# A depthwise convolution whose shared tap sum moves from VectorE to ScalarE and GpSimd

## The chip, the core and the metric

One core of one Trainium2 chip runs the whole model in one launch. The metric is the device time of that launch in microseconds (us). The engines are named as the profile names them: PE (TensorE matmul), PEld (its weight load), DVE (VectorE), ACT (ScalarE), POOL (GpSimd) and SP (which issues the DMAs). Each works through a list of its own in a fixed order and waits where an operand or a buffer is not ready.

## What is computed

A decoder of two layers over 1024 positions of 1024 features. The change lies in the first layer's convolution block. The reference, cut to it:

```
def conformer_conv(h, w_pw1, b_pw1, w_dw, b_dw, ln_g, ln_b, w_pw2, b_pw2):
    u = h @ w_pw1 + b_pw1
    a, gate = jnp.split(u, 2, axis=-1)
    u = a * jax.nn.sigmoid(gate)
    u = depthwise causal convolution of u over time, 31 taps per feature, + b_dw
    u = jax.nn.silu(layernorm(u, ln_g, ln_b))
    return u @ w_pw2 + b_pw2
```

The rest of the model (cross-attention into 256 memory tokens, two MLPs, one attention layer) follows it and is not touched. Some of the cross-attention's preparation depends on weights and memory tokens alone: for each of 2 layers and 4 heads, two products of weight matrices (the code calls the whole `memory_matrices`, this text "prep").

## The kernel before

Features lie on the 128 partitions, positions along the free axis, so the 1024 features make 8 chunks (`m`, `NCH`) and the positions two halves of 512 (`HALVES`).

For each chunk `gated_unit` computes the gate: per half two products of 24 matmuls (the gate's, then the linear part's; f32 numbers are split into a high and a low part, hence three passes over 8 blocks), each into one of the two banks of `pm`. ACT takes the sigmoid of the first (`sg`, L368) and DVE combines it with the second into `u` (L370). A chunk of `u` is stored as even and odd positions (`u[:, 0]`, `u[:, 1]`), with 15 zero columns in front.

`convolve` makes the 31 taps with 512-column instructions, in the form that saves multiplications: with differences `d0`, `d1` of even and odd positions (L393, L394), and one sum that both outputs share,

- `both` = bias + the 16 pair sums of taps times the odd positions: one TENSOR_SCALAR (L396) and 15 SCALAR_TENSOR_TENSORs on DVE (L400), each adding to the one before;
- output half `s=0` (even outputs): `both` + 16 taps over `d0`; `s=1`: `both` + 15 taps over `d1`, all on DVE (L408), accumulated in place in `X[:, m, HALVES[s]]` in SBUF.

The two outputs are added into `acc[0]`, `acc[1]` (L354), whose partition means start the layer norm after the last chunk: `token_mean` and `spread` are small PE products (L158, L167), with DVE, ACT and POOL steps between. Then `linear` multiplies by `pw2` (384 matmuls of 512 columns), and `add_x` (L324) leaves the new residual.

Prep is a generator: `conv_layer` calls it for 4 pieces of work before and 2 more in each chunk. For one head it makes 32 products `mem,praw` (64 matmul records: an f32 product runs as two), 16 `kt,praw` and 8 `praw,vt`, in PSUM banks of its own (`pps`, 4 banks), which ACT empties into `o` tiles (L483, L501; two buffers each) that SP stores to DRAM.

No order is written out by hand in this stage. A scheduler goes through the program in the order in which the code traced it, keeps its own estimate of when operands are ready, and gives each engine the ready instruction that was traced first. The result is a fixed list for each engine.

Of the kernel before, what the change touches and what calls it, by code (L numbers as in the profile page):

```python
# [12 lines left out]
F32 = mybir.dt.float32  # L13
F32R = mybir.dt.float32r
AF = mybir.ActivationFunctionType
ALU = mybir.AluOpType
# [3 lines left out]
P = 128  # L20
D = 1024
S = 1024
NCH = D // P
HALF = 512
# [6 lines left out]
TAPS = 31  # L31
PAD = TAPS - 1
# [4 lines left out]
HALVES = (slice(0, HALF), slice(HALF, S))  # L37
# [49 lines left out]
def trunk(ctx, tc, a, out):  # L87
    nc = tc.nc
    act, dve, pool, pe = nc.scalar, nc.vector, nc.gpsimd, nc.tensor
# [14 lines left out]
    def col(name, i):  # L104
        return par[:, COLS[name] + i : COLS[name] + i + 1]
# [30 lines left out]
    X = open_x()  # L136
    nrm = ctx.enter_context(tc.tile_pool(name="nrm", bufs=2))
# [3 lines left out]
    def bank(p):  # L141
        return p.tile([P, HALF], F32, name="mm", tag="mm")

    def banks(n):
        return tc.tile_pool(name="pm", bufs=n, space=PSUM, reuse_waits="tile")
# [144 lines left out]
        dve.tensor_tensor(X[:, m, sl], t, X[:, m, sl], op=ALU.add)  # L290


    def conv_layer(pm, prep):
        with tc.tile_pool(name="conv", bufs=2) as cp:
            for sl in HALVES:
                next(prep)
# [34 lines left out]
            hs = operands()  # L331
            ahead = gate_weights(0)
            u = padded()
            for sl in HALVES:
                normalize(hs, "mix0", sl)
                next(prep)
                gated_unit(pm, cp, 0, ahead, hs, u[:, :, PAD // 2 :], sl)
            acc = [cp.tile([P, HALF], F32, name=f"acc{s}", bufs=1) for s in range(2)]
            for m in range(NCH):
                if m:  # L340
                    u = padded()
                    for sl in HALVES:
                        gated_unit(pm, cp, m, ahead, hs, u[:, :, PAD // 2 :], sl)
                if m + 1 < NCH:
                    ahead = gate_weights(m + 1)
                for _ in range(2):
                    next(prep, None)

                convolve(cp, m, u, pairs[:, m])
                for s, sl in enumerate(HALVES):  # L350
                    if m == 0:
                        act.copy(acc[s], X[:, m, sl])
                    else:
                        dve.tensor_tensor(acc[s], acc[s], X[:, m, sl], op=ALU.add)  # L354
# [7 lines left out]
    def gated_unit(pm, cp, m, ws, hs, u, sl):  # L362
        sg = cp.tile([P, HALF], F32, name="sg")
        for j, w in zip((1, 0), ws):
            t = bank(pm)
            product(t, by_weights(w, hs, sl))
            if j:
                act.activation(sg, t, AF.Sigmoid, bias=col("pw1_b", NCH + m))  # L368
            else:
                dve.scalar_tensor_tensor(  # L370
                    u[:, :, sl.start // 2 : sl.stop // 2],
                    t.rearrange("p (n s) -> p s n", s=2), col("pw1_b", m),
                    sg.rearrange("p (n s) -> p s n", s=2), op0=ALU.add, op1=ALU.mult,
                )
# [8 lines left out]
        dve.tensor_tensor(sums[:, :, :n], two[:, :, :, 0], two[:, :, :, 1], op=ALU.add)  # L383
        return sums

    def convolve(cp, m, u, sums):


        n, k = S // 2, TAPS // 2
        even, odd = u[:, 0, :], u[:, 1, :]  # L390
        d0 = cp.tile([P, n + k], F32, name="d0")
        d1 = cp.tile([P, n + k - 1], F32, name="d1")
        dve.tensor_tensor(d0, even[:, : n + k], odd[:, : n + k], op=ALU.subtract)  # L393
        dve.tensor_tensor(d1, even[:, 1 : n + k], odd[:, : n + k - 1], op=ALU.subtract)  # L394
        both = cp.tile([P, n], F32, name="both")
        dve.tensor_scalar(  # L396
            both, odd[:, :n], sums[:, 0:1], col("dw_b", m), op0=ALU.mult, op1=ALU.add
        )
        for j in range(1, k + 1):
            dve.scalar_tensor_tensor(  # L400
                both, odd[:, j : j + n], sums[:, j : j + 1], both, op0=ALU.mult, op1=ALU.add
            )
        out = [X[:, m, sl] for sl in HALVES]
        for s, d, taps in ((0, d0, k + 1), (1, d1, k)):
            y = both
            for j in range(taps):
                w = col("dw_w", m * TAPS + 2 * j + s)
                dve.scalar_tensor_tensor(  # L408
                    out[s], d[:, j : j + n], w, y, op0=ALU.mult, op1=ALU.add
                )  # L410
                y = out[s]

# [15 lines left out]
    @contextmanager  # L428
    def prep_pools(n):
        with tc.tile_pool(name="prep", bufs=2) as pp, tc.tile_pool(name="pps", bufs=n, space=PSUM) as pq:  # L430
            yield pp, pq
# [1014 lines left out]
```

## Time and profile before

| | us |
|---|---|
| median of 3 runs (2818.59 to 2823.66) | 2822.05 |
| the profiled execution | 2825.31 |
| its span on the engines | 2823.3 |
| PE busy | 2740.8 (97%) |
| DVE busy | 2030.9 (72%) |
| ACT busy | 1278.3 (45%) |
| POOL busy | 703.1 (25%) |

Times in the trace count from the start of the span. The convolution block takes the stretch from 0 to about 526 us: the last `add_x` starts at 525.5. A busy share is an average over stages with different limits, so the prediction looks at this stretch alone. Of a row that groups instructions, the numbers behind the bar are busy time (us), mean duration (ns), and, behind a second bar, the engine's idle time before them with what ended it. Instructions of one engine can overlap at their ends: busy time divided by count is then below the mean duration.

### The profile page before, as it was taken

What the parts mean: (1) busy time and instruction counts of PE and PEld (TensorE: products, weight loads), DVE (VectorE), ACT (ScalarE), POOL (GpSimd) and SP (SyncE); (2) the same over time, 40 slices, a digit from 0 to 9 for tenths busy, and PEclk for the clock granted to TensorE, in tenths of its full rate; (3) what the DMA queues carried; (4) which work ended last, traced back from release to release, by engine and by line L of the source; (5) the groups of instructions that cost most, each with busy time, mean ns of one, the idle gap of its engine ahead of it and who ended that gap; (6) DMA issues with size and microseconds to landing.
All of it is one profiled execution on the core that took longest, in us unless ns stands there. A gap on an engine that the chain in (4) does not pass through costs nothing.

```text
span 2823.3 us, 36214 instructions
## 1 busy us (share of the span) xinstructions
PE 2740.8 (97%) x12968; PEld 2261.3 (80%) x12968; DVE 2030.9 (72%) x3358; ACT 1278.3 (45%) x2293; POOL 703.1 (25%) x473
## 2 busy tenths in 40 slices
PE   8999999999999999999899999989999999989998
PEld 6777777888888877888688888878888788878886
DVE  5999984555776576777788888875546855577776
ACT  5212143433555553333466666673423655543332
POOL 0000000000065625774000000000000365525773
PEclk9999999999999999999899999999999999999999
DMA  6334364322165585652222221243213455655651
GB/s 219 120 119 135 114 206 124 101 90 70 65 230 177 178 309 187 227 199 89 69 68 70 57 65 55 69 136 98 94 64 105 149 176 190 218 208 197 227 201 61
DMA packets 165428, 390.68 MB, mean 138 GB/s; under 512 B 17264, under 2 KB 46192, under 8 KB 164992
## 3 DMA queue, kind: packets, MB, share of 16 engines
q1 hardware_dynamic: 165248, 388.37, 40.9%
q8 instruction: 102, 1.67, 0.2%
q14 instruction: 78, 0.64, 0.1%
HBM read 270.79 MB, written 113.31 MB: 136 GB/s over the span
## 4 chain that ended last, share of the span: by engine, by line
PE 74%; DVE 12%; ACT 5%; DMA 5%; issue 3%; POOL 1%; SPq 0%; DVEq 0%; POOLq 0%; ACTq 0%
PE mm L1070 34%; PE mm L269 29%; PE mm L1255 5%; DVE w L148 2%; DVE op L148 2%; DVE x L408 1%; PE mm L1341 1%; DVE x L1310 1%; DMA ua<-x 1%; ACT x L1315 1%; PE mm L1353 1%; PE mm L1354 1%; DVE both L400 1%; DVE wl L148 1%; ACT pth L151 1%
## 5 line engine op out<-in xcount | busy, mean ns | idle before, releaser
L1070 PE MATMUL mm<-op,w 128*128 128x512 f32 x5424 | 1242.4, 391 | 24.5 <-ACT m L955 8.7
L1070 PEld LDWEIGHTS mm<-op,w 128*128 128x128 f32 x5424 | 1020.5, 189 | 243.2 <-ACT m L955 9.6
L269 PE MATMUL mm<-op,wh 128*128 128x512 f32 x1056 | 330.5, 394 | 4.2 <-DVE op L148 4.2
L148 DVE TENSOR_TENSOR w<-r,w 128x512 fp32r<-128x512 f32 x264 | 262.6, 998 | 30.5 <-ACT w L653 30.5
L653 ACT CAST w<-r 128x512 fp32r<-128x512 f32 x264 | 163.3, 622 | 262.0 <-PE mm L1070 233.2
L269 PEld LDWEIGHTS mm<-op,wh 128*128 128x128 f32 x1056 | 200.2, 190 | 48.5 <-DVE op L148 6.5
L1255 PE MATMUL mm<-op,wh 128*128 128x512 f32 x736 | 231.4, 396 | 0.0
L148 DVE TENSOR_TENSOR w<-t,w 128x512 fp32r<-128x512 f32 x180 | 178.2, 1005 | 63.2 <-ACT w L653 63.1
L269 PE MATMUL mm<-op,wl 128*128 128x512 f32 x528 | 210.5, 400 | 7.1 <-DVE wl L148 6.2
L207 POOL TENSOR_TENSOR r<-v,mhalf 128x4 f32<-128x4 f32 (+1 forms) x15 | 16.8, 1117 | 741.0 <-DVE v L205 741.0
L647 POOL TENSOR_TENSOR t<-r,t 128x512 f32<-128x512 f32 x104 | 174.9, 1681 | 91.4 <-DVE w L148 54.2
L653 ACT CAST w<-t 128x512 fp32r<-128x512 f32 x180 | 112.0, 622 | 169.8 <-PE mm L1070 140.6
L151 ACT CAST wh<-raw 128x1024 fp32r<-128x1024 f32 x96 | 100.7, 1050 | 193.8 <-PE mm L269 97.5
L865 POOL TENSOR_TENSOR x<-x,x 128x512 f32<-128x512 f32 x112 | 160.2, 1455 | 112.6 <-ACT x L878 101.6
L967 DVE TENSOR_TENSOR x<-mm,x 128x512 f32<-128x512 f32 x160 | 109.5, 684 | 91.1 <-PE mm L1070 73.7
L1255 PEld LDWEIGHTS mm<-op,wh 128*128 128x128 f32 x736 | 139.2, 189 | 26.7
L269 PE MATMUL mm<-op,xsh 128*128 128x512 f32 x512 | 158.0, 393 | 0.0
L1255 PE MATMUL mm<-op,wl 128*128 128x512 f32 x368 | 155.0, 421 | 1.9 <-ACT q L1275 1.9
L151 ACT CAST pth<-mm 128x512 fp32r<-128x512 f32 (+1 forms) x224 | 105.9, 495 | 108.5 <-PE mm L556 80.8
L408 DVE SCALAR_TENSOR_TENSOR x<-d,par,x 128x512 f32<-128x512 f32 x232 | 154.5, 746 | 0.0
L647 POOL TENSOR_TENSOR t<-r,r 128x512 f32<-128x512 f32 x52 | 80.2, 1542 | 295.1 <-DMA r<-in_ff_w 191.0
L1315 ACT ACTIVATE x<-x,nb 128x128 f32<-128x128 f32 (+7 forms) x128 | 99.5, 778 | 109.3 <-DVE nb L1313 100.0
(188 smaller groups left out, 4689.6 us busy)
## 6 DMA issues: line engine op xcount, KB each, us to landing
r<-in_ff_w SPq DMA_DIRECT2D x128, 512.0 KB, 4.0
op<-ua SPq DMA_DIRECT2D x80, 512.0 KB, 6.8
us<-x SPq DMA_DIRECT2D x128, 256.0 KB, 2.9
op<-us SPq DMA_DIRECT2D x64, 512.0 KB, 5.6
raw<-mvo SPq DMA_DIRECT2D x32, 512.0 KB, 3.4
ua<-ul SPq DMA_DIRECT2D x64, 256.0 KB, 2.2
ua<-uh SPq DMA_DIRECT2D x60, 256.0 KB, 2.3
raw<-in_pw SPq DMA_DIRECT2D x24, 512.0 KB, 4.7
```

What stands on the lines that cost most here:

```text
L148: dve.tensor_tensor(lo, src, hi.bitcast(F32), op=ALU.subtract)
L151: act.copy(hi, src)
L269: pe.matmul(out_ps, x, y, start=i == 0, stop=i == len(terms) - 1)
L400: dve.scalar_tensor_tensor(both, odd[:, j : j + n], sums[:, j : j + 1], both, op0=ALU.mult, op1=ALU.add)
L408: dve.scalar_tensor_tensor(out[s], d[:, j : j + n], w, y, op0=ALU.mult, op1=ALU.add)
L647: (dve if g in (2, 3, UP, UP + 1) else pool).tensor_tensor(t, raws[g, x], raws[g, y], op=ALU.subtract)
L653: act.copy(highs[n][0], raws[steps[n][:2]])
L865: eng.tensor_tensor(u[g, x], y1, y2, op=op_)
L967: dve.tensor_tensor(v, sums[key], v, op=ALU.add)
L1070: pe.matmul(sums[key], y, z, start=first and i == 0, stop=n == last_of[key] and i == len(terms) - 1, skip_group_check=True,)
L1255: pe.matmul(t, x, y, start=n == 0, stop=n == len(terms) - 1)
L1315: act.activation(x[:, :n], x[:, :n], AF.Exp, bias=nb, accum_out=rs)
```

## The change

1. The shared sum gets a function of its own, `shared_sum`. ACT computes the bias and first product (L398) and 15 products `tap` (L401, four buffers); POOL adds each to `both` (L402), 15 additions in a row. DVE's L396 and L400 are gone.
2. In `convolve` the running sum of both outputs is one PSUM bank (`acc`, from the new pool `pc`; "mm" in the lists). Only the last tap of each output writes `X`. `d0` and `d1` have one buffer instead of two.
3. The gate of chunk m+1 and its shared sum are traced ahead of the filters of chunk m.
4. Prep has 3 PSUM banks instead of 4.

```
     def conv_layer(pm, pc, prep):
...
             acc = [cp.tile([P, HALF], F32, name=f"acc{s}", bufs=1) for s in range(2)]
+            ready = u, shared_sum(cp, 0, u, pairs[:, 0])
             for m in range(NCH):
-                if m:
-                    u = padded()
-                    for sl in HALVES:
-                        gated_unit(pm, cp, m, ahead, hs, u[:, :, PAD // 2 :], sl)
+                now = ready
+
                 if m + 1 < NCH:
                     ahead = gate_weights(m + 1)
                 for _ in range(2):
                     next(prep, None)
-
-                convolve(cp, m, u, pairs[:, m])
+                if m + 1 < NCH:
+                    u = padded()
+                    for sl in HALVES:
+                        gated_unit(pm, cp, m + 1, ahead, hs, u[:, :, PAD // 2 :], sl)
+                    ready = u, shared_sum(cp, m + 1, u, pairs[:, m + 1])
+
+                convolve(cp, pc, m, *now)
...
+    def shared_sum(cp, m, u, sums):
+        n, k = S // 2, TAPS // 2
+        odd = u[:, 1, :]
+        both = cp.tile([P, n], F32, name="both")
+        act.activation(both, odd[:, :n], AF.Identity, scale=sums[:, 0:1], bias=col("dw_b", m))
+        for j in range(1, k + 1):
+            t = nrm.tile([P, HALF], F32, name="tap", tag="t", bufs=4)
+            act.activation(t, odd[:, j : j + n], AF.Copy, scale=sums[:, j : j + 1])
+            pool.tensor_tensor(both, both, t, op=ALU.add)
+        return both
+
+    def convolve(cp, pc, m, u, both):
...
+        d0 = cp.tile([P, n + k], F32, name="d0", bufs=1)
+        d1 = cp.tile([P, n + k - 1], F32, name="d1", bufs=1)
...
+        acc = bank(pc)
         for s, d, taps in ((0, d0, k + 1), (1, d1, k)):
             y = both
             for j in range(taps):
+                o = X[:, m, HALVES[s]] if j == taps - 1 else acc
                 w = col("dw_w", m * TAPS + 2 * j + s)
-                dve.scalar_tensor_tensor(
-                    out[s], d[:, j : j + n], w, y, op0=ALU.mult, op1=ALU.add
-                )
-                y = out[s]
+                dve.scalar_tensor_tensor(o, d[:, j : j + n], w, y, op0=ALU.mult, op1=ALU.add)
+                y = acc
...
-    with prep_pools(4) as pools, banks(2) as pm:
-        conv_layer(pm, chain(*(memory_matrices(*pools, l) for l in range(2))))
+    with prep_pools(3) as pools, banks(2) as pm, banks(1) as pc:
+        conv_layer(pm, pc, chain(*(memory_matrices(*pools, l) for l in range(2))))
```

Lines below it shift by 8: `add_x` stays L324, `gated_unit`'s L368 and L370 become L372 and L374, prep's L483 and L501 become L491 and L509.

The scheduler's lists move in three places. On DVE, before, between the filters of chunk 0 and of chunk 1 (`x00`, `x01` are the two outputs of chunk 0, `x10`, `x11` of chunk 1, `u_678` is chunk 1's gated input, its two rows the two halves):

```order
L408 SCALAR_TENSOR_TENSOR x01_78<-d1_625,par_63,x01_78 128x512 [waits DVE_49]
L408 SCALAR_TENSOR_TENSOR x00_77<-d0_624,par_63,x00_77 128x512 [waits DVE_49]
L370 SCALAR_TENSOR_TENSOR u_678<-mm_707,par_63,sg_680 128x2x256 [waits PE_49,Activation_49]
L370 SCALAR_TENSOR_TENSOR u_678<-mm_760,par_63,sg_733 128x2x256 [waits PE_49,Activation_49]
L148 TENSOR_TENSOR wl_789<-raw_786,wh_788 128x1024 [waits DMAHW1_49,Activation_49]
L148 TENSOR_TENSOR wl_795<-raw_792,wh_794 128x1024 [waits DMAHW2_49,Activation_49]
L393 TENSOR_TENSOR d0_866<-u_678 128x527 [waits DVE_49]
L394 TENSOR_TENSOR d1_867<-u_678 128x526
L396 TENSOR_SCALAR both_870<-u_678,sums_227,par_63 128x512
L400 SCALAR_TENSOR_TENSOR both_870<-u_678,sums_227,both_870 128x512 [waits DVE_49] x15
L408 SCALAR_TENSOR_TENSOR x10_79<-d0_866,par_63,both_870 128x512 [waits DVE_49]
L408 SCALAR_TENSOR_TENSOR x11_80<-d1_867,par_63,both_870 128x512
```

The same engine now, from the last tap of output 0 of chunk 0 to the first of chunk 1 (`u_674` is chunk 1's gated input; `mm_833` the running sum; a row's "waits Pool" is its wait for `both`):

```order
L418 SCALAR_TENSOR_TENSOR x00_77<-d0_829,par_63,mm_833 128x512 [waits DVE_49]
L418 SCALAR_TENSOR_TENSOR mm_833<-d1_830,par_63,both_569 128x512 [waits DVE_49]
L374 SCALAR_TENSOR_TENSOR u_674<-mm_703,par_63,sg_676 128x2x256 [waits PE_49,Activation_49]
L418 SCALAR_TENSOR_TENSOR mm_833<-d1_830,par_63,mm_833 128x512 [waits DVE_49] x8
L148 TENSOR_TENSOR wl_870<-raw_867,wh_869 128x1024 [waits DMAHW1_49,PE_49,Activation_49]
L418 SCALAR_TENSOR_TENSOR mm_833<-d1_830,par_63,mm_833 128x512 [waits DVE_49] x3
L374 SCALAR_TENSOR_TENSOR u_674<-mm_756,par_63,sg_729 128x2x256 [waits PE_49]
L418 SCALAR_TENSOR_TENSOR mm_833<-d1_830,par_63,mm_833 128x512 [waits DVE_49]
...
L410 TENSOR_TENSOR d0_1102<-u_674 128x527
L418 SCALAR_TENSOR_TENSOR x01_78<-d1_830,par_63,mm_833 128x512 [waits DVE_49]
L411 TENSOR_TENSOR d1_1103<-u_674 128x526 [waits DVE_49]
L418 SCALAR_TENSOR_TENSOR mm_1106<-d0_1102,par_63,both_782 128x512 [waits Pool_49]
```

The two outputs' taps alternated before and now stand one chain behind the other. The next chunk's second half of `u` stands near the end of the second chain, three taps and two differences ahead of the row that needs the next `both`. The later chunks repeat this, with 27 or 28 filter taps (191 over the seven passages) between the wait for one `both` and the second half of the next `u`.

On ACT, before, where one chunk's `sg` is followed by prep's `o` tiles:

```order
L368 ACTIVATE sg<-mm,par 128x512 [waits DVE_49,PE_49] x2
L151 CAST wh<-raw 128x1024 [waits DMAHW6_49,DVE_49]
L483 ACTIVATE o<-mm,par 128x256 [waits DMAHW3_49,PE_49]
L151 CAST wh<-raw 128x1024 [waits DMAHW7_49,DVE_49,PE_49]
L483 ACTIVATE o<-mm,par 128x256 [waits PE_49]
```

and now, the same kind of place:

```order
L151 CAST wh<-raw 128x1024 [waits DMAHW2_49,DVE_49,PE_49]
L491 ACTIVATE o<-mm,par 128x256 [waits PE_49]
L398 ACTIVATE both<-u,par,sums 128x512 [waits DVE_49]
L401 ACTIVATE tap<-u,sums 128x512 [waits Pool_49] x15
L491 ACTIVATE o<-mm,par 128x256 [waits PE_49]
L491 ACTIVATE o<-mm,par 128x256 [waits DMAHW0_49]
L372 ACTIVATE sg<-mm,par 128x512 [waits PE_49]
```

Most of prep's `o` tiles and the next chunk's `sg` now stand behind 15 taps, which wait for POOL to free their four buffers.

On PE, before, from the mean of the second output's filters (`acc_565`) to the first product of `pw2` (`op,wl`):

```order
L158 MATMUL mm<-mean_col,acc_565 128x1 x4
L269 MATMUL mm<-mem,praw 128x256 x3
L167 MATMUL mm<-ident,nm 128x128 x4
L269 MATMUL mm<-mem,praw 128x256 x29
L269 MATMUL mm<-kt,praw 128x256 x12
L269 MATMUL mm<-praw,vt 128x512
L158 MATMUL mm<-mean_col,acc 128x1 x4
...
L269 MATMUL mm<-kt,praw 128x256 x4
L269 MATMUL mm<-praw,vt 128x512
L269 MATMUL mm<-op,wl 128x512 x2
```

and now from the same mean (`acc_568`):

```order
L158 MATMUL mm<-mean_col,acc_568 128x1 x4
L269 MATMUL mm<-kt,praw 128x256
L269 MATMUL mm<-praw,vt 128x512
L167 MATMUL mm<-ident,nm 128x128 x4
L269 MATMUL mm<-praw,vt 128x512 x5
L269 MATMUL mm<-mem,praw 128x256 x3
L158 MATMUL mm<-mean_col,acc 128x1 x4
...
L269 MATMUL mm<-mem,praw 128x256 x28
L269 MATMUL mm<-kt,praw 128x256 x12
L269 MATMUL mm<-praw,vt 128x512 x2
L269 MATMUL mm<-kt,praw 128x256 x2
L269 MATMUL mm<-op,wl 128x512
```

Behind the means of the first filters (`acc_564`, `acc_567`) before and now, prep has 32 and 92 `mem,praw`, 28 and 48 `kt,praw`, and 16 and 24 `praw,vt` rows left (a row of these lists is two records of the trace). Between the second mean and the second sum of squares, the row before had 32 `mem,praw`, 12 `kt,praw` and 1 `praw,vt`, and now has 3, 1 and 6.

More of the change, by code (lines that the diff above doesn't have):

```diff
@@ L290, in add_to_x, with conv_layer @@
         dve.tensor_tensor(X[:, m, sl], t, X[:, m, sl], op=ALU.add)
-    def conv_layer(pm, prep):
+    def conv_layer(pm, pc, prep):
         with tc.tile_pool(name="conv", bufs=2) as cp:
@@ L384, in tap_sums @@
         return sums
-    def convolve(cp, m, u, sums):
+    def shared_sum(cp, m, u, sums):
[9 more added lines that the diff above has]
+    def convolve(cp, pc, m, u, both):
         n, k = S // 2, TAPS // 2
         even, odd = u[:, 0, :], u[:, 1, :]
-        d0 = cp.tile([P, n + k], F32, name="d0")
-        d1 = cp.tile([P, n + k - 1], F32, name="d1")
+        d0 = cp.tile([P, n + k], F32, name="d0", bufs=1)
+        d1 = cp.tile([P, n + k - 1], F32, name="d1", bufs=1)
         dve.tensor_tensor(d0, even[:, : n + k], odd[:, : n + k], op=ALU.subtract)
         dve.tensor_tensor(d1, even[:, 1 : n + k], odd[:, : n + k - 1], op=ALU.subtract)
-        both = cp.tile([P, n], F32, name="both")
-        dve.tensor_scalar(
-            both, odd[:, :n], sums[:, 0:1], col("dw_b", m), op0=ALU.mult, op1=ALU.add
-        )
[L399 to L403, printed above, removed]
+        acc = bank(pc)
         for s, d, taps in ((0, d0, k + 1), (1, d1, k)):
```

2 lines of the change are left out of this document (removed).

## The prediction

> **What bounds the kernel now.** I read the busy times by stretch first, to see which engine fills the convolution block, then the groups of DVE, then the chain that ended last. The stretches are: the filters of chunks 0 to 6, chunk 7, the layer norm, and `pw2` (columns: us, then busy time and count of PE, PEld, DVE, ACT, POOL).
>
> ```profile
> core 0: us, PE busy (x) PEld busy (x) DVE busy (x) ACT busy (x) POOL busy (x), PEclk, DMA share, GB/s
> 76.00:349.00 273.00, 269.34 (x1142) 213.95 (x1141) 268.09 (x386) 56.14 (x91) 0.75 (x6) 1.00 0.38 120
> 349.00:389.00 40.00, 39.01 (x164) 30.49 (x162) 39.44 (x57) 8.54 (x16) 0.00 (x0) 1.00 0.76 243
> 389.00:434.00 45.00, 44.22 (x209) 34.07 (x210) 33.66 (x57) 30.20 (x55) 2.01 (x2) 1.00 0.61 192
> 450.00:520.00 70.00, 70.00 (x311) 57.97 (x310) 23.41 (x29) 12.73 (x18) 0.00 (x0) 1.00 0.32 94
> ```
>
> PE and DVE are both full while the filters run. PE's idle time from 76 to 434 is 3.7 + 1.0 + 0.8 = 5.4 us, and none in the last row. 70.0 us for 311 matmuls is 0.225 us for one of 512 columns, so it runs at its pace too. DVE sets when the filters end, but PE loses nothing by it, since it does prep in the meantime. So a faster DVE can give this block at most about 5 us; what the change can do on a large scale is take work away from PE at the right moment, that is, make it wait.
>
> The groups of DVE in the block, and the times of L396, the first step of each chunk's shared sum (min/median/max ns, first and last start):
>
> ```profile
> L408 DVE SCALAR_TENSOR_TENSOR x<-d,par,x 128x512 f32<-128x512 f32 x232 | 154.5, 746 | 0.0
> L400 DVE SCALAR_TENSOR_TENSOR both<-u,sums,both 128x512 f32<-128x512 f32 x120 | 90.2, 752 | 4.1
> L370 DVE SCALAR_TENSOR_TENSOR u<-mm,par,sg 128x512 f32<-128x512 f32 x16 | 11.6, 747 | 2.9 <-PE mm L269 2.9
> L354 DVE TENSOR_TENSOR acc<-acc,x 128x512 f32<-128x512 f32 x14 | 9.0, 686 | 0.0
> L148 DVE TENSOR_TENSOR wl<-raw,wh 128x1024 fp32r<-128x1024 f32 x26 | 31.1, 1220 | 12.5 <-ACT wh L151 12.1 <-DMA x<-in_xT 0.4
> L396 DVE TENSOR_SCALAR both<-u,sums,par x8: 536/542/552, 79.1 to 353.1; 128x512 f32<-128x512 f32 x8
> ```
>
> A chunk takes (353.1 - 79.1) / 7 = 39.1 us. Two rates stand in the first rows. L408 alternates between two outputs, and each tap costs 154.5 / 232 = 0.666 us. L400 adds to its own last result, and each step costs (90.2 + 4.1) / 120 = 0.786 us: it must wait until the one before has written.
>
> **The change: DVE's share.** L396 and L400 leave DVE, 0.54 + 15 x 0.786 = 12.3 us a chunk. The taps stay, 31 a chunk, but the two chains no longer alternate: each tap reads the running sum that the tap before wrote. So they go at the dependent rate. That the sum lies in PSUM has no row of its own; 0.666 (independent) is the floor, and a DVE operation beside POOL, below, is the ceiling. I take 0.786, the row of the same instruction in a dependent chain. [...]
>
> **POOL's and ACT's share.** One shared sum is now two ACT instructions and then 15 POOL additions, each on the result of the last. The rows nearest to them: ACT with scale and bias per partition (L318), ACT with a scale per partition (L501), and eight POOL additions partly dependent on each other, from the timeline, beside which DVE ran three instructions; below them a single POOL addition, and the dearest group.
>
> ```profile
> L318 ACT ACTIVATE x<-x,par 128x512 f32<-128x512 f32 x16 | 12.1, 806 | 0.0
> L501 ACT ACTIVATE o<-mm,mem_r 128x512 f32<-128x512 f32 x32 | 21.8, 686 | 51.8 <-DMA mqk<-o 25.0 <-DMA mvo<-o 20.3 <-PE mm L269 5.9
> 842.54 11.41 POOL L865 TENSOR_TENSOR x<-x,x 128x512 f32<-128x512 f32 x8
> 2623.46 1.30 POOL L924 TENSOR_TENSOR x<-x,x 128x512 f32<-128x512 f32 x1
> L647 POOL TENSOR_TENSOR r<-r 128x512 f32<-128x512 f32 x52 | 87.2, 1697 | 0.0
> ```
>
> 11.41 / 8 = 1.43 us a step; I take it since the new sum will stand beside three or four DVE instructions too (`wl`, `d0`, `d1`). Bounds are 1.30 and 1.70. A shared sum takes 0.81 + 0.69 + 15 x 1.43 = 22.9 us from the moment `u` is complete, nearly twice DVE's 12.3.
>
> **Whether it is hidden.** It would be, had it a whole chunk of filters to run beside. Tracing ahead should give it that, but DVE's list decides, and there the second half of the next `u` (without which no position sum can start) stands 27 or 28 taps behind the wait for this chunk's `both`, and three taps ahead of the wait for the next. So the two sums form one loop: `both` ready, 191 / 7 = 27.3 taps, two `u` steps, one `acc` addition, one `wl`, then ACT and POOL, then the next `both`. One turn is 27.3 x 0.786 = 21.5, plus 2 x 0.75 + 0.69 + 1.22 = 3.4, plus 22.9: 47.8 us, against 39.1 before. DVE waits for POOL for most of the 21.4.
>
> PE's work for a chunk is 96 x 0.225 = 21.6 us of gate, and one piece of prep. These rows price prep by start to next start:
>
> ```profile
> 408.47 12.68 PE L269 MATMUL mm<-mem,praw 128*128 128x256 f32 x58
> 421.00 5.50 PE L269 MATMUL mm<-kt,praw 128*128 128x256 f32 x24
> ...
> 368.61 3.60 PE L269 MATMUL mm<-praw,vt 128*128 128x512 f32 x8
> 372.04 3.62 PE L269 MATMUL mm<-mem,praw 128*128 128x256 f32 x16
> ```
>
> 12.53 / 58 = 0.216 us a record, so 0.43 a `mem` or `kt` row of the order; 3.43 / 8 = 0.43, so 0.86 a `vt` row. A piece of prep (32 `mem`, or 16 `kt` and 8 `vt`) is 13.8 us, and a chunk 35.4 us of PE. In a turn of 47.8, PE idles 12: its next linear product needs the bank that DVE empties only behind the first chain, and prep's `o` tiles stand on ACT behind taps that wait for POOL. The one PSUM bank less of prep costs nothing that this wait does not cover.
>
> **The end of the block.** The first `u` was complete, and its `wh` cast done, at 77.0:
>
> ```profile
> 75.94 1.05 ACT L151 CAST wh<-raw 128x1024 fp32r<-128x1024 f32 x1 [3.81 <-PE mm L269]
> 75.94 0.75 DVE L370 SCALAR_TENSOR_TENSOR u<-mm,par,sg 128x512 f32<-128x512 f32 x1 [2.56 <-PE mm L269]
> ```
>
> So the first `both` comes at 77.0 + 22.9 = 99.9, the eighth at 99.9 + 7 x 47.8 = 434.5. Its first chain, one tap more and the `acc` addition (12.6 + 0.8 + 0.7) bring the first mean to 448.6. In the chain that ended last, that mean, the first and the second variance stand so:
>
> ```profile
> 389.03 1.05 PE mm L158 x8
> ...
> 402.27 0.80 PE mm L158 x8
> ...
> 404.40 1.16 PE mm L167 x8
> ...
> 427.40 0.80 PE mm L158 x8
> ```
>
> From here three terms:
>
> 1. The first mean is 448.6 - 389.0 = 59.6 us late.
> 2. Prep left behind it is 60 `mem`, 20 `kt` and 8 `vt` rows more than before: 80 x 0.43 + 8 x 0.86 = 41.3 us of PE that the loop's gaps did not take.
> 3. From 404.4 to 427.4 DVE and ACT needed 23.0 us for the second variance, and PE had prep for all of it. Now its list has 4 rows of 0.43 and 6 of 0.86 there, with the small products (three of about 1 us) some 10: it waits 13 us for the product that follows. Ahead of the first variance there is no such wait: 28 `mem`, 14 `kt` and 2 `vt` rows, 19.8 us with the small products some 21, against 13.2 before plus 13 taps that now mix in, 8 to 10 us.
>
> The L501 row also shows ACT waiting for stores to free `o`. Two heads of prep now follow each other with hardly a matmul of `pw2` between, so I add 5 us (0 to 10). Sum: 59.6 + 41.3 + 13 + 5 = 119 us. What follows the block is unchanged. The profiled execution's own 2825.3 (span 2823.3) becomes 2944; it lies 3.3 above the median of the runs, and against that median I forecast 2941.
>
> Bounds: with 1.30 and 0.666 a turn is 42.6 and the eighth `both` comes at 396; the mean is 40 us earlier than reckoned, 2901, and 2883 without terms 3's wait and the stores. With 1.70 for POOL alone, 8 x 15 x 0.27 = 32 us more, 2973.
>
> **Rivals.** *The sum is hidden.* Should the loop not close, because POOL's sum runs beside the taps as the tracing intends, DVE needs some 25 + 6 us a chunk, less than PE's 35.4, and PE's 5.4 us of idle time is all there is to gain: 2817, or just about what a measurement can tell from no change. It decides where the second `u` half reaches ACT a full 23 us ahead of the next `both`'s first use; the list leaves three taps and two differences, some 4 us. Chance 0.07, split between faster and same. The case that the change does not do what it says, tracing ahead without running ahead, is my forecast itself.
>
> *PE fills the gaps with prep.* With 7 x 12.4 = 87 us of prep drawn into them, only 32 of the 119 remain: 2854. Its list of one piece of prep a chunk speaks against it. Chance 0.05.
>
> *The taps collide with POOL.* DVE rows of the same operation and size, in the MLPs beside POOL, and in this block without it:
>
> ```profile
> L148 DVE TENSOR_TENSOR w<-r,w 128x512 fp32r<-128x512 f32 x264 | 262.6, 998 | 30.5 <-ACT w L653 30.5
> L148 DVE TENSOR_TENSOR op<-h,op 128x512 fp32r<-128x512 f32 x16 | 10.9, 689 | 0.5 <-ACT op L222 0.4
> ```
>
> If each tap paid those 0.31 us, 191 of them make 59 and the forecast 3000. The loop speaks against it: taps and additions hardly overlap. [...] Chance 0.06.
>
> **The numbers.** The loop has 0.82. Its range, 2880 to 2980, holds both bounds of POOL's step and the floor of the tap's; it leaves out the three rivals (0.18) and 0.02 of the loop. A measurement of this kernel can tell about 0.2% (5.6 us) from no change. Faster by more: 0.04, the hidden sum. Within: 0.03. Slower: 0.93.
>
> **What would show it.** Right: L396 of before, now ACT's L398, starts every 47 to 48 us; POOL's L402 steps come 1.4 us apart, with DVE idle for 15 us or more a chunk until POOL ends; the taps lie 0.79 apart; PE's busy share between 76 and 400 falls to about three quarters; the first mean comes at about 449 and the last `add_x` near 645, where before it began at 525.5. Wrong: L398 every 35 us and DVE waiting for PE instead (the hidden sum); more than one piece of prep in a turn; taps of 1 us while POOL runs. Taps well under 0.75 would say that a sum in PSUM is cheaper to reuse than one in SBUF.

## The result and the profile after

| | before | after |
|---|---|---|
| median of the runs | 2822.86 us | 2935.41 us |
| ratio, 95% interval | | 1.0398 [1.0372, 1.0424] |
| profiled execution, own time (span) | 2825.3 (2823.3) us | 2927.21 (2925.4) us |
| mean of the first filters (L158), start | 389.0 us | 440.5 us |
| last mean behind the block, start | 538.6 us | 647.7 us |

Slower by 112.6 us of median, where the prediction's sum was 119 (2941). The block is 647.7 - 538.6 = 109.1 us longer in the profiled executions. The whole span is 102.1 us longer, so what follows the block won back 7 us in that execution.

The turn of the loop, as the starts of ScalarE's first step of each shared sum (min/median/max ns, first and last start):

```profile
L398 ACT ACTIVATE both<-u,par,sums x8: 812/814/816, 74.5 to 403.4; 128x512 f32<-128x512 f32 x8
```

(403.4 - 74.5) / 7 = 47.0 us; it was 39.1. One turn on three engines, from the timelines (start, us, engine and line, count, and in brackets the idle time before and what ended it), VectorE first, then ScalarE, then GpSimd:

```profile
143.63 0.76 DVE L418 SCALAR_TENSOR_TENSOR mm<-d,par,both 128x512 f32<-128x512 f32 x1 [17.37 <-POOL both L402]
144.43 11.05 DVE L418 SCALAR_TENSOR_TENSOR mm<-d,par,mm 128x512 f32<-128x512 f32 x14
...
166.88 0.75 DVE L374 SCALAR_TENSOR_TENSOR u<-mm,par,sg 128x512 f32<-128x512 f32 x1
...
174.06 1.77 DVE L411 TENSOR_TENSOR d<-u 128x526 f32<-128x526 f32 x1
175.76 0.68 DVE L474 TENSOR_TENSOR kt<-mm,mem_rs 128x512 f32<-128x512 f32 x1
190.67 0.76 DVE L418 SCALAR_TENSOR_TENSOR mm<-d,par,both 128x512 f32<-128x512 f32 x1 [14.23 <-POOL both L402]
```

```profile
167.66 0.81 ACT L398 ACTIVATE both<-u,par,sums 128x512 f32<-128x512 f32 x1 [0.99 <-DVE u L374]
```

```profile
169.16 21.47 POOL L402 TENSOR_TENSOR both<-both,tap 128x512 f32<-128x512 f32 x15 [25.51 <-ACT tap L401]
```

From the first tap to the second half of the next gated input and ScalarE's start: 167.66 - 143.63 = 24.0 us. From there through the products and 15 additions to the next first tap: 190.67 - 167.66 = 23.0 us. GpSimd idles 25.5 us while the taps run, VectorE 14.2 while the additions run: the two take turns instead of working side by side.

What VectorE and TensorE waited for in the block (engine, line, what ended the wait: us in all, times, longest):

```profile
DVE mm L418 <- POOL both L402: 120.8, 8, 17.4
...
PE mm L269 <- ACT o L491: 48.7, 6, 19.0
...
PE mm L269 <- DVE u L374: 31.9, 4, 8.9
...
PE mm L269 <- ACT o L509: 10.9, 2, 10.3
```

TensorE is what ends the block, so its time is the one to balance. With every row, its waits from 75 to 680 us are 96.8 us, 6.6 before. But they are not all. These five groups hold the same matmuls in both kernels (group, count, busy us, mean ns, idle before); first before, then after:

```profile
L269 PE MATMUL mm<-op,wh 128*128 128x512 f32 x768 | 237.8, 391 | 0.0
L269 PE MATMUL mm<-op,wl 128*128 128x512 f32 x384 | 152.3, 398 | 1.7 <-DVE wl L148 1.7
L269 PE MATMUL mm<-mem,praw 128*128 128x256 f32 x512 | 116.7, 386 | 9.1 <-ACT mem L451 8.7 <-DMA praw<-in_mem_wk 0.5
...
L269 PE MATMUL mm<-kt,praw 128*128 128x256 f32 x256 | 61.2, 385 | 6.0 <-ACT o L483 4.5 <-DMA praw<-in_mem_wq 1.4
L269 PE MATMUL mm<-praw,vt 128*128 128x512 f32 x128 | 59.1, 594 | 0.0
```

```profile
L269 PE MATMUL mm<-op,wh 128*128 128x512 f32 x768 | 243.7, 399 | 0.0
L269 PE MATMUL mm<-op,wl 128*128 128x512 f32 x384 | 157.6, 410 | 31.9 <-DVE u L374 31.9
L269 PE MATMUL mm<-mem,praw 128*128 128x256 f32 x512 | 118.2, 390 | 9.6 <-ACT mem L459 8.9 <-ACT o L509 0.6
L269 PE MATMUL mm<-kt,praw 128*128 128x256 f32 x256 | 68.9, 420 | 52.4 <-ACT o L491 50.5 <-DMA praw<-in_mem_wq 1.9
L269 PE MATMUL mm<-praw,vt 128*128 128x512 f32 x128 | 62.0, 621 | 10.3 <-ACT o L509 10.3
```

The same matmuls are busy for 650.4 instead of 627.1 us. Waits and slower matmuls together are 90.2 + 23.3 = 113.5 us, against a block longer by 109.1. The slower matmuls stand in stretches with a granted clock below 1.00: the gate's `op,wh` products have a mean of 405 ns in the first stretch below, at 0.91, and of 389 in the last, at 1.00. The stretches (us, then busy time and count of PE, PEld, DVE, ACT, POOL, granted clock, DMA share, GB/s) are the filters of chunks 0 to 6, chunk 7, the second variance and the rest of `pw2`:

```profile
76.00:403.00 327.00, 267.06 (x1077) 211.13 (x1075) 212.02 (x269) 123.65 (x189) 141.46 (x111) 0.91 0.28 90
403.00:440.50 37.50, 15.08 (x42) 8.66 (x40) 22.30 (x28) 16.25 (x26) 20.48 (x15) 0.73 0.36 106
...
464.60:487.80 23.20, 12.89 (x45) 8.05 (x46) 19.75 (x32) 18.63 (x30) 0.00 (x0) 0.71 0.36 102
...
521.00:634.00 113.00, 112.60 (x486) 90.74 (x484) 31.56 (x39) 26.08 (x39) 0.00 (x0) 1.00 0.37 112
```

In the three stretches in which TensorE is kept waiting it is also granted less clock, 0.91, 0.73 and 0.71, where the prediction's rows of before had 1.00 throughout.

### The profile page after: what moved, and what is told of

Same layout as the page of the kernel before. It is cut to its first block, busy times and chain, and to the rows that moved or that the text cites. A ratio compares the mean times of both kernels' runs of the same rounds, so it can differ in the third digit from the quotient of the medians.

```text
span 2925.4 us, 36412 instructions
## 1 busy us (share of the span) xinstructions
PE 2755.8 (94%) x12968; PEld 2268.0 (78%) x12968; DVE 1972.9 (67%) x3230; ACT 1365.5 (47%) x2421; POOL 867.6 (30%) x593
## 4 chain that ended last, share of the span: by engine, by line
PE 66%; DVE 14%; ACT 6%; POOL 6%; issue 4%; DMA 3%; SPq 0%; POOLq 0%; DVEq 0%; ACTq 0%
PE mm L1078 34%; PE mm L269 21%; POOL both L402 5%; DVE mm L418 5%; PE mm L1263 5%; DVE op L148 2%; DVE w L148 1%; PE mm L1349 1%; DVE x L1318 1%; ACT x L1323 1%; PE mm L1361 1%; PE mm L1362 1%; DVE wl L148 1%; PE mm L1313 1%; PE mm L1314 1%
## 5 line engine op out<-in xcount | busy, mean ns | idle before, releaser
L269 PE MATMUL mm<-op,wl 128*128 128x512 f32 x528 | 215.9, 409 | 37.4 <-DVE u L374 31.9
L402 POOL TENSOR_TENSOR both<-both,tap 128x512 f32<-128x512 f32 x120 | 161.6, 1346 | 217.9 <-ACT tap L401 209.1
L975 DVE TENSOR_TENSOR x<-mm,x 128x512 f32<-128x512 f32 x160 | 109.5, 685 | 90.3 <-PE mm L1078 70.8
L418 DVE SCALAR_TENSOR_TENSOR mm<-d,par,mm 128x512 f32<-128x512 f32 x216 | 163.0, 755 | 6.0
```

What stands on the lines that cost most here:

```text
L269: pe.matmul(out_ps, x, y, start=i == 0, stop=i == len(terms) - 1)
L402: pool.tensor_tensor(both, both, t, op=ALU.add)
L418: dve.scalar_tensor_tensor(o, d[:, j : j + n], w, y, op0=ALU.mult, op1=ALU.add)
L975: dve.tensor_tensor(v, sums[key], v, op=ALU.add)
```

## The experiments

Two theories went into the first four runs. **The loop:** the next gate stands behind the taps on VectorE, the additions behind the gate, the next taps behind the additions. **The rival:** the running sum in PSUM, the dependent taps and the bank taken from preparation. What the runs left open led to a third, **ScalarE's queue**: TensorE is starved by evictions that stand behind the products there. All figures in one table (each ratio is taken against executions of before made beside that run, which is why it can differ a little from the quotient of two medians; then the mean of the first filters, the last mean behind the block, TensorE's waits from 75 to 680 us, the busy time of the five groups above, VectorE's wait for GpSimd's sum):

| run | median us | ratio [95%] | first mean | last mean | PE waits | five groups | DVE waits |
|---|---|---|---|---|---|---|---|
| before | 2822.9 | 1 | 389.0 | 538.6 | 6.6 | 627.1 | - |
| after | 2935.4 | 1.0398 [1.0372, 1.0424] | 440.5 | 647.7 | 96.8 | 650.4 | 120.8 |
| sum_on_dve | 2833.8 | 1.0043 [1.0019, 1.0067] | 386.3 | 547.8 | 16.3 | 628.4 | - |
| sum_not_ahead | 2915.0 | 1.0327 [1.0299, 1.0355] | 446.8 | 626.9 | 73.0 | 650.9 | 156.1 |
| taps_in_sbuf | 2927.1 | 1.0375 [1.0341, 1.0408] | 442.9 | 641.2 | 90.3 | 649.5 | 141.4 |
| two_ahead | 2906.7 | 1.0311 [1.0273, 1.0350] | 391.4 | 619.8 | 71.0 | 646.7 | 53.2 |
| eight_products | 2937.3 | 1.0407 [1.0383, 1.0430] | 439.0 | 648.3 | 92.8 | 654.4 | 120.8 |
| two_ahead_eight | 2897.2 | 1.0264 [1.0245, 1.0282] | 378.3 | 608.3 | 56.3 | 649.0 | 53.2 |
| ten_steps | 2903.9 | 1.0282 [1.0264, 1.0300] | 403.4 | 611.9 | 60.0 | 651.2 | 85.1 |
| five_steps | 2844.5 | 1.0082 [1.0057, 1.0106] | 353.8 | 558.0 | 23.0 | 635.2 | 42.9 |
| gate_early | 2900.1 | 1.0280 [1.0253, 1.0307] | 395.1 | 614.4 | 62.9 | 633.7 | 18.9 |
| gate_early_evict | 2888.9 | 1.0237 [1.0219, 1.0256] | 390.7 | 602.7 | 54.5 | 635.1 | 18.9 |
| three_banks | 2838.0 | 1.0059 [1.0042, 1.0075] | 386.5 | 553.4 | 19.4 | 630.9 | - |
| gate_early_sbuf | 2943.6 | 1.0415 [1.0392, 1.0438] | 442.0 | 657.0 | 99.7 | 639.3 | 123.2 |

The balance made above (waits and the five groups, each over before) comes within about 5 us of the block's lengthening in every run, but for the three named gate_early, where it is 8 to 13 us short. There the busy time of the five groups grows by 7 to 12 us, but mean duration times count by 18 to 27 us; with that the balance closes to within about 3 us.

**sum_on_dve.** After, with the shared sum on VectorE again:

```
-        act.activation(both, odd[:, :n], AF.Identity, scale=sums[:, 0:1], bias=col("dw_b", m))
+        dve.tensor_scalar(
+            both, odd[:, :n], sums[:, 0:1], col("dw_b", m), op0=ALU.mult, op1=ALU.add
+        )
...
-            t = nrm.tile([P, HALF], F32, name="tap", tag="t", bufs=4)
-            act.activation(t, odd[:, j : j + n], AF.Copy, scale=sums[:, j : j + 1])
-            pool.tensor_tensor(both, both, t, op=ALU.add)
+            dve.scalar_tensor_tensor(
+                both, odd[:, j : j + n], sums[:, j : j + 1], both, op0=ALU.mult, op1=ALU.add
+            )
```

> The changed kernel, but the shared sum is back on VectorE as 1 + 15 instructions; running sum in PSUM, one preparation bank less, gate traced ahead all stay. The loop theory: no other engine is in the loop, so the turn is VectorE's own work, the 39.1 us of the kernel before with 31 taps at 0.786 instead of 0.666 us, about 42.8 us: 8 x 3.7 = 30 us over the kernel before, 2845 to 2860 us. Rival, PSUM, the bank or the tracing ahead is the cause: it stays near 2935 us.

2833.8 us: the move of the shared sum to two other engines is about 100 of the 113 us, and the rival falls as the main cause. The expectation was still too high, since it let the taps go at the dependent rate of 0.786. The timeline shows why they did not:

```profile
159.93 0.75 DVE L420 SCALAR_TENSOR_TENSOR mm<-d,par,mm 128x512 f32<-128x512 f32 x1
160.59 0.75 DVE L402 SCALAR_TENSOR_TENSOR both<-u,sums,both 128x512 f32<-128x512 f32 x1
161.25 0.75 DVE L420 SCALAR_TENSOR_TENSOR mm<-d,par,mm 128x512 f32<-128x512 f32 x1
...
168.32 3.92 DVE L420 SCALAR_TENSOR_TENSOR mm<-d,par,mm 128x512 f32<-128x512 f32 x5
```

Traced ahead, the next shared sum alternates with this chunk's taps, two chains that do not depend on each other: (161.25 - 159.93) / 2 = 0.66 us a step, against 3.92 / 5 = 0.78 where a chain runs alone.

**sum_not_ahead.** Before, with the sum's instructions alone moved to ScalarE and GpSimd (the same lines the other way round, in the kernel before):

> The kernel before with one part of the change alone: the shared sum on ScalarE and GpSimd, everything else as before (not traced ahead, taps alternating between the halves in SBUF, four preparation banks). The loop theory: VectorE waits for the whole sum in each chunk, a turn of 1.5 + 21.5 (sum) + 31 x 0.666 = 20.6 (taps) + about 5 (gates, differences, accumulations) = 48 to 49 us, 2930 to 2960 us: tracing ahead bought next to nothing. Rival, tracing ahead did hide part of the sum: clearly slower than the changed kernel, above 2960 us; rival, PSUM and the bank are the cause: 2822 to 2850 us.

2915.0 us, a little less than expected and less than after. VectorE waits 156.1 us for the sums instead of 120.8, yet the whole is 20 us faster than with tracing ahead, PSUM and one bank less. The next run, taps_in_sbuf, differs from this one by tracing ahead, and by one buffer instead of two for `d0` and `d1`, and takes 2927.1 us. The two intervals overlap: tracing ahead, as it stands, bought nothing.

**taps_in_sbuf.** After, with the running sum in `X` and four banks for preparation:

```
-        acc = bank(pc)
...
-                o = X[:, m, HALVES[s]] if j == taps - 1 else acc
+                o = X[:, m, HALVES[s]]
...
-                y = acc
+                y = o
...
-    with prep_pools(3) as pools, banks(2) as pm, banks(1) as pc:
+    with prep_pools(4) as pools, banks(2) as pm:
```

> The changed kernel, but the running sum is kept in X in SBUF (two chains that alternate, as before) and preparation has its four banks again; shared sum on ScalarE and GpSimd, traced ahead. The loop theory: taps are shorter (0.666 us), but the gate's second half now stands behind all 31 taps of the chunk instead of 27: 31 x 0.666 + 4.4 (gates, accumulations, weight share) + 1.5 + 21.5 = 48 us a turn, no better than the changed kernel: 2925 to 2945 us. Rival, the dependent taps and the lost bank carry a good part of the loss: 31 x 0.12 x 8 = 30 us less or more, 2905 us or below.

2927.1 us, as the loop theory had it. The interval overlaps that of after, so these parts are worth little while the loop stands.

**two_ahead.** After, with gates and sums traced two chunks ahead (the same loop body, `u` and `both` with `bufs=3`):

```
-                if m + 1 < NCH:
-                    ahead = gate_weights(m + 1)
+                for n in (1, 2) if m == 0 else (m + 2,):
+                    if n < NCH:
+                        ahead = gate_weights(n)
...
+                        ready.append((u, shared_sum(cp, n, u, pairs[:, n])))
```

> The changed kernel, but a chunk's gate and shared sum are traced two chunks ahead instead of one (u and both with three buffers). The loop theory (the next gate sits behind 27 of 31 taps on VectorE, the 15 GpSimd additions behind the gate, the next taps behind the additions): the gate's second half now stands after tap 12 of chunk 0 and then after taps 4, 6, 12, 17, 22 and 28 of chunks 1 to 6, so the 22.9 us of a shared sum are covered by what is left of the taps in the early chunks and by little in the late ones. VectorE's wait for GpSimd falls from 120.8 us to about 8+0+1+6+9+13+18 = 55 us, the time to about 2870 us. Rival, the running sum in PSUM and the bank that it takes (or additions slowed by the other engines) are the cause: nothing changes, 2935 us.

VectorE's wait came out as worked out (expected 55), the time did not (2906.7 for 2870):

```profile
DVE mm L418 <- POOL both L402: 53.2, 5, 18.8
...
PE mm L269 <- ACT o L491: 38.7, 3, 18.1
...
PE mm L269 <- ACT sg L372: 16.3, 2, 8.9
```

The filters end at 391.4, practically where they end in the kernel before, and the block still ends 81 us later. The loop alone cannot be the whole account: TensorE waits 71.0 us in this kernel too, and what it did not do beside the filters it does behind them.

**eight_products and two_ahead_eight.** After, and two_ahead, with buffers of their own for ScalarE's products:

```
-            t = nrm.tile([P, HALF], F32, name="tap", tag="t", bufs=4)
+            t = cp.tile([P, HALF], F32, name="tap", bufs=8)
```

> The changed kernel, but ScalarE's products for the shared sum have eight buffers of their own in place of four shared ones; the order on every engine is the same. What the run two chunks ahead left open: TensorE waits for evictions of its preparation products that stand behind the 15 products in ScalarE's queue, and those are held back by GpSimd's pace. With eight buffers ScalarE is through with its 15 products after about 11 us instead of 21. Theory of ScalarE's queue: the turn of the loop (27 taps, gate, 15 additions) stays at 47 us and the filters end at about 440 us as before, but TensorE's 48.7 us of waits for those evictions fall by half or more, so that less preparation is left for after the filters: 2895 to 2915 us. Theory of the loop alone: no change, 2930 to 2940 us.

> Two chunks ahead, and eight buffers for ScalarE's products. Theory of ScalarE's queue: two chunks ahead already ended the filters at 391 us, the time of the kernel before, and what is left of its loss is TensorE's waiting, 38.7 us of it for the evictions behind the products; with those gone most of it goes: 2865 to 2885 us. Theory that something else starves TensorE there (the order of its own queue, in which the next gate's products stand behind preparation): 2895 to 2907 us, no change that counts.

In eight_products the wait for the evictions did halve, and another took its place:

```profile
PE mm L269 <- DVE u L374: 41.0, 7, 9.5
...
PE mm L269 <- ACT o L491: 25.1, 5, 12.1
```

41.0 + 25.1 = 66.1 us against 31.9 + 48.7 = 80.6, but with every row 92.8 against 96.8, and a turn of (401.8 - 72.9) / 7 = 47.0: no change in time. The edit did what it was for: ScalarE's products wait for GpSimd for 18.0 us in all (28 times), in after for 56.1 (80 times). So in the changed kernel ScalarE's queue is covered by the loop. Two chunks ahead, where the loop is partly open, the same edit brings 1.0311 to 1.0264, some 13 us with intervals that just overlap, where 22 to 42 were expected. The 2897.2 us lie in the range of the other theory, that the order of TensorE's own queue starves it, which no run tests by itself. The theory of ScalarE's queue holds at most as a smaller term behind the loop.

**ten_steps and five_steps.** After, with the last 5 or 10 of a chunk's 15 products and additions left out, so that the filters lack those terms (`for j in range(1, 11)` and `range(1, 6)`):

> The changed kernel with 10 instead of 15 additions on GpSimd a chunk (the products 11 to 15 of the shared sum are left out, on ScalarE too). The gate's second half now stands behind all 31 taps. The loop theory: 31 x 0.786 = 24.4, two gates, two accumulations and a weight share about 4.4, ScalarE's 1.5, 10 x 1.43 = 14.3: a turn of 44.6 us instead of 47.0, 7 x 2.4 + 7.2 = 24 us less: about 2911 us, and less again where ScalarE's queue is freed 7 us earlier in each chunk, down to 2885 us. If the additions had nothing to do with it: 2935 us.

> The changed kernel with 5 instead of 15 additions on GpSimd a chunk (products 6 to 15 left out). The loop theory: a turn of 24.4 + 4.4 + 1.5 + 7.15 = 37.5 us, below the 39.1 us of the kernel before: the filters end by 375 us and TensorE, with its 35.4 us of work a chunk, is again nearly full: 2830 to 2855 us. If the additions had nothing to do with it: 2935 us.

Turns of (373.5 - 73.4) / 7 = 42.9 and, from the row below, 36.8 us (expected 44.6 and 37.5), 2903.9 and 2844.5 us. The loss follows the length of the chain: 113, 81, 21 us for 15, 10, 5 additions. The edit takes as many products out of ScalarE's queue, so these two runs alone do not tell the loop from that queue; eight_products, where the queue was freed sooner and nothing was gained, speaks for the loop.

```profile
L398 ACT ACTIVATE both<-u,par,sums x8: 812/814/817, 73.1 to 330.8; 128x512 f32<-128x512 f32 x8
```

With five, the turn is about TensorE's 35.4 us of work a chunk, and it waits 23.0 us in all. The 21 us that remain are about what the bank alone costs, below.

**gate_early and gate_early_evict.** After, with the next gate ahead of preparation and by priority; then also with the `o` tiles on VectorE and eight buffers for the products:

```
+                        with tc.high_priority(offset=500):
+                            gated_unit(pm, cp, m + 1, ahead, hs, u[:, :, PAD // 2 :], sl)
...
+                for _ in range(2):
+                    next(prep, None)
```

```
-                        act.activation(o[:, f, :], t[:, f, :], AF.Copy, scale=gain)
+                        dve.tensor_scalar(o[:, f, :], t[:, f, :], gain, None, op0=ALU.mult)
```

> The changed kernel, but the next chunk's gate is put ahead of the preparation and of the taps by priority: its second half now stands after taps 0 to 22 of the chunk, from the second chunk on often more than a chunk ahead. The loop theory (and the condition that the prediction gave for its rival of a hidden sum): the additions run beside the taps, VectorE's wait for GpSimd, 120.8 us, falls to below 40, and the filters end near 350 us; the time falls below the 2897 us of two chunks ahead with eight buffers, to 2860 to 2890 us, since TensorE still waits for evictions behind ScalarE's products. If an early gate does not hide the additions: 2920 to 2940 us.

> The gate by priority as in the run before, and ScalarE taken out of TensorE's way: the preparation's evictions (the o tiles) on VectorE, and eight buffers for ScalarE's products. Theory of ScalarE's queue as what is left: TensorE's waits in the block fall to some 20 us, as where GpSimd had five additions: 2830 to 2855 us. If the order of TensorE's own queue, or VectorE, which now has the evictions too, starves it: 2865 us or more.

In gate_early VectorE's taps wait for GpSimd's sum in the first chunk only, and the time is still 2900 us:

```profile
DVE wl L148 <- ACT wh L151: 48.6, 13, 10.3
...
PE mm L269 <- ACT sg L373: 39.3, 11, 7.3
...
DVE mm L419 <- POOL both L403: 18.9, 1, 18.9
...
PE mm L269 <- ACT o L492: 13.4, 9, 3.9
```

The filters end at 395.1, not near 350. VectorE now waits longest for `wh`, ScalarE's cast of the next weights, which stands behind the products that GpSimd paces: 46.5 of the 48.6 us fall between 60 and 450 us, 36.2 more than in the kernel before (10.3). By its length that is most of the 45 us. So GpSimd's pace still reaches VectorE, by way of ScalarE. TensorE now waits for `sg`, the sigmoid of the next gate, which ScalarE has behind the products that GpSimd paces. With evictions off ScalarE and eight buffers, 2888.9 us: better, but far from the 2830 to 2855 expected. There VectorE, which now has the evictions too, is busy for 232 of the 280 us from 75 to 355, and TensorE waits 22.3 us for them and 11.9 for `u`. No single wait is left that explains the 68 us that remain. That part stays open; that some order of the same instructions reaches the kernel before was not shown.

**three_banks.** Before, with `prep_pools(3)` in place of `prep_pools(4)`:

> The kernel before with three preparation banks in PSUM instead of four, nothing else. The prediction's step that the lost bank costs nothing: 2820 to 2826 us, ratio within 1.001. Rival, the bank is what is left of the loss when the shared sum goes back to VectorE (1.0043): 1.003 to 1.005, 2831 to 2837 us.

1.0059 [1.0042, 1.0075], 17 us, for one bank. It is as much as sum_on_dve loses in all (1.0043 [1.0019, 1.0067]), so the bank is enough to explain that rest, and dependent taps need no price there.

```profile
PE mm L269 <- ACT o L501: 8.8, 2, 7.7
PE mm L269 <- ACT o L483: 4.1, 6, 1.9
```

**gate_early_sbuf.** gate_early with the edit of taps_in_sbuf:

> The run with the gate by priority, but with the running sum in X in SBUF and four preparation banks, as in the kernel before. It asks what the running sum in PSUM buys once taps do run beside GpSimd's additions. If a tap with both tensors in SBUF collides with GpSimd as the differences and the first taps do there (0.7 to 1.6 us, 0.75 to 1.75 us): taps that run beside an addition take 1.0 to 1.7 us each, and with some 80 to 120 of the 248 taps there the filters last 20 to 80 us longer, 2905 to 2960 us. If taps do not collide: their mean stays at 0.75 us, and the bank that comes back and the alternating chains make it faster than the 2900 us with the sum in PSUM, 2870 to 2895 us.

2943.6 us. Here is the one place where the running sum in PSUM earns its keep. Taps beside GpSimd's additions, first in gate_early (sum in PSUM, additions from 248.0 to 269.6), then here (sum in SBUF, additions from 112.1 to 137.8):

```profile
248.26 1.62 DVE L411 TENSOR_TENSOR d<-u 128x527 f32<-128x527 f32 x1
249.81 7.87 DVE L419 SCALAR_TENSOR_TENSOR mm<-d,par,mm 128x512 f32<-128x512 f32 x10
```

```profile
110.49 2.73 DVE L418 SCALAR_TENSOR_TENSOR x<-d,par,x 128x512 f32<-128x512 f32 x4
...
113.74 25.23 DVE L418 SCALAR_TENSOR_TENSOR x<-d,par,x 128x512 f32<-128x512 f32 x16
```

0.79 us a tap with the sum in PSUM, 25.23 / 16 = 1.58 with it in SBUF, where the four taps just before the additions took 0.68 each. The time is not this alone: the scheduler also put the gates later here, behind 20 to 31 taps in all chunks but the first, and VectorE waits 123.2 us again.

## Why the prediction was right

**The loop.** Right, and nearly to the microsecond: 24.9 us from the sum to ScalarE's start against 24.0, 22.9 through ScalarE and GpSimd against 23.0, a turn of 47.8 against 47.0. The 1.43 us a step that it chose for GpSimd is 21.47 / 15 = 1.43. The chain of work that ended last, for the last chunk, shows what is in that mean (start, us, what):

```profile
406.20 2.13 POOL both L402
...
409.75 1.59 POOL both L402
...
414.44 1.26 POOL both L402
415.78 1.26 POOL both L402
```

1.34 us from start to start (415.78 - 414.44) when VectorE is idle; of the steps beside its `wl`, accumulation and difference (405.2 to 411.9) three last 1.59 to 2.13 us, the steps behind them 1.26 or 1.27. That was the reason the prediction gave. That the loss comes from the moved sum is shown by sum_on_dve, and that it follows the length of this chain by the steps left out. TensorE's share of the filters fell to 267.06 / 327 = 0.82, not to the three quarters forecast; part of that busy time is longer matmuls: the 672 products of the gate (`op,wh` and `op,wl`) that stand there were busy for 238.3 us, at a granted clock of 0.91, where they had 227.4 at 1.00 before.

**The taps.** 0.786 forecast; 11.05 / 14 = 0.79 measured. The sum in PSUM cost nothing beside the dependent rate of before's chain in SBUF. That this rate would hold for it was the author's estimate; two rows of before pointed the same way, L370, which reads PSUM and lasts 747 ns, and L408, which does not and lasts 746.

**The first mean.** +59.6 forecast, 440.5 - 389.0 = 51.5 measured: seven turns shorter by 0.8 us, and a first sum that starts 2.5 us sooner.

**Behind the filters.** +59.3 us forecast (41.3 preparation left, 13 of wait, 5 for stores). The wait for a store to free an `o` tile stands in the chain as foreseen (4.2 us of DMA from 514.2), but it cost TensorE 0.6 us, not 5. The wait ahead of the second variance came, with another releaser:

```profile
468.68 2.74 PE L269 MATMUL mm<-praw,vt 128*128 128x512 f32 x6
481.72 3.78 PE L269 MATMUL mm<-praw,vt 128*128 128x512 f32 x4 [10.30 <-ACT o L509]
```

TensorE does not wait 13 us for the variance but 10.3 for a preparation bank, whose eviction stands behind ScalarE's part of the layer norm. The reason of that term holds all the same: the stretch lasted 23.2 us (464.6 to 487.8) where the prediction had 23.0, VectorE's last sum for the second variance ends at 487.0, and TensorE had work for 12.9 us of it (10 forecast). The bank's wait fell into time in which TensorE would have idled anyway. From the first mean to the start of the last `add_x` (633.4 now, 525.5 before) TensorE is busy 44.7 us longer than before (180.4 against 135.7) and idle 11.7 us longer (12.5 against 0.8), 56.4 in all. With the first mean that is 51.5 + 56.4 = 107.9 us where 119 was forecast: 633.4 stands where the prediction had near 645. Behind the block, where the prediction had no change, 7 us were won back. The profiled execution is the fastest of the four and 102 us slower than before's; that the median, 112.6, lies nearer to the forecast is in part chance.

**What it lacked.** The clock is in none of its terms. The two rows above are the same instruction: 2.74 / 6 = 0.46 us a record ahead of the idle 10.3 us, where the granted clock was 1.00 (468.6 to 471.5), 3.78 / 4 = 0.95 behind it, where it was 0.50 (481.7 to 485.6). In the whole block a lower granted clock is the likely source of the 23.3 us of longer matmuls; no run separates it from other causes. It was not missed in the total because the prediction took idle and lost time in the turn by its length, which holds both.

**The bank.** "Costs nothing that this wait does not cover" held: with the bank back, taps_in_sbuf is within the interval of after. Without the loop to cover it, the bank costs 17 us, which the prediction did not say.

**The rivals.** The taps did not collide with GpSimd, for two reasons: they hardly run beside it in the changed kernel, and where they do with the sum in PSUM, in gate_early, they take 0.79 us. With the sum, their second input, in SBUF too, in gate_early_sbuf, they took 1.58, and in after the rows with two inputs in SBUF, some of which stand beside the additions (L358 lasts 1.54 us at 172.60, beside them, and 0.69 at 157.49, without them), are longer than before (L354 had 686 ns; the first row is before's L394, which became L411):

```profile
L394 DVE TENSOR_TENSOR d<-u 128x526 f32<-128x526 f32 x8 | 5.6, 702 | 0.0
```

```profile
L418 DVE SCALAR_TENSOR_TENSOR mm<-d,par,mm 128x512 f32<-128x512 f32 x203 | 153.2, 755 | 6.0
...
L358 DVE TENSOR_TENSOR acc<-acc,x 128x512 f32<-128x512 f32 x13 | 13.6, 1045 | 0.2
L411 DVE TENSOR_TENSOR d<-u 128x526 f32<-128x526 f32 x8 | 13.5, 1684 | 0.0
```

The rival of the hidden sum was priced wrongly, as far as gate_early shows it. It said that with the second half of `u` 23 us ahead of need, the time would be 2817. In gate_early the taps wait for a sum once, and the time is 2900. A sum hidden from the taps still holds ScalarE's queue: VectorE needs that queue for `wh` (36.2 us more of waits than in the kernel before), TensorE for `sg` and its `o` banks (39.3 and 13.4 us). With part of that taken out the time was still 2889 (gate_early_evict), so this does not account for all of the gap; 17 us of it are what the missing bank cost alone. Preparation did not fill the gaps (the other rival): TensorE's list was as fixed as the prediction read it.

## What to carry to other kernels

Before work is moved to an idle engine, follow its result round: if the consumer's own list holds the input of the next round behind this round's consumption, the two engines take turns, and the new chain counts at its full length (23.0 us for 12.3 taken away). Then ask which queue the moved work now sits in and who else lives on it; here breaking the first loop gave back 35 of 113 us, and the products still held `wh`, `sg` and evictions that feed VectorE and TensorE; part of the rest stays open. Look at idle time of TensorE for more than its length: here about a fifth of the loss (23.3 of 113.5 us) was matmuls that took longer, in stretches with a granted clock of 0.91, 0.73 and 0.71.

## What the hardware showed that was not expected

- One preparation bank of PSUM less cost 17 us (0.59%) in a kernel whose TensorE had 6.6 us of waits.
- Two dependent chains of VectorE that alternate ran at 0.66 us a step and one alone at 0.78, in sum_on_dve, where one of the two lies in PSUM.
- Taps and additions side by side were both slower: beside taps with two SBUF inputs, 15 additions on GpSimd took 25.64 us in gate_early_sbuf, against 21.59 in gate_early beside taps with the sum in PSUM:

```profile
248.03 21.59 POOL L403 TENSOR_TENSOR both<-both,tap 128x512 f32<-128x512 f32 x15 [17.33 <-ACT both L399]
```

```profile
112.12 25.64 POOL L403 TENSOR_TENSOR both<-both,tap 128x512 f32<-128x512 f32 x15 [10.21 <-ACT tap L402]
```
